# Expert stage of a diffusion block: the order of TensorE's work written by hand, the second product one expert late

## The chip, the cores and the metric

One core of one Trainium2 chip runs the whole kernel as one program. The metric is the device time of one execution in microseconds (us); lower is better. "The time before" is the median of three runs.

## The reference, cut to what matters

One layer: a token mixer for 256 tokens of width 1024 (its code is left out, the change doesn't touch it), then a mixture of 32 experts in which each token goes to 4, and a last norm. All weights are float32; each expert has `w1` (1024 x 2048, 8 MB) and `w2` (1024 x 1024, 4 MB), so that the stage reads 384 MB from HBM.

```python
def moe_ffn(h, w_router, b_router, w1, b1, w2, b2):
    ...
    top_logit, top_e = lax.top_k(logits, TOP_K)
    top_w = jax.nn.softmax(top_logit, axis=-1)
    ...
    def expert_block(args):
        xblk, e = args
        z = xblk @ w1[e] + b1[e]
        gate = jnp.minimum(z[:, :D_EXPERT], SWIGLU_LIMIT)
        lin = jnp.clip(z[:, D_EXPERT:], -SWIGLU_LIMIT, SWIGLU_LIMIT)
        return (gate * jax.nn.sigmoid(SWIGLU_ALPHA * gate) * (lin + 1.0)) @ w2[e] + b2[e]
    ...
    out = jnp.zeros((n_tok + 1, d), hf.dtype).at[slot_tok].add(
        (y * slot_w[:, None]).astype(hf.dtype))[:n_tok]
...
        x = x + g2 * moe_ffn(modulate(x, norm2_g[layer], sh2, sc2), *ffn_w)
    return rms_norm(x, final_g)
```

## The kernel before

The expert stage begins at about 504 us of the profile, after the mixer and the router. The loop of line 879 runs over the 32 experts; each has 64 token slots. For one expert:

- `gather` (lines 762 to 775): a product of the tokens with a 0/1 matrix (`select`) puts the expert's tokens in its slots, transposed, in two halves (`k4`). It is made for two experts at once, so a half is 16 matmul instructions; DVE and ACT move it from PSUM to `xT2` with scale and shift.
- `spread` (lines 777 to 783): one small product and a compare make the matrix `pT` that takes slots back to tokens.
- `expert_in` (lines 785 to 813): the bias of `w1` opens the banks `gate` and `lin` (line 791); eight weight tiles of 1 MB are loaded (line 795) and multiplied (line 798); the clamped SwiGLU runs on DVE and ACT (lines 803 to 807); TensorE turns the result by four transposes (line 810), and ACT copies it to `hT2` (line 812).
- `expert_out` (lines 815 to 843): the bias opens `py` (line 820), four tiles of `w2` are loaded (line 824) and multiplied (line 828), DVE makes `y` (line 831), and for each half `tt` of the tokens a product scatters it (line 840) and DVE adds it to `acc` (line 843). The last expert goes through `expert_out_by_columns` (lines 845 to 866), 256 columns of `w2` at a time (rows of 1 KB), and the final norm follows (lines 958 to 969).

A matmul in float32 is two MATMUL instructions in the profile, and `w1` and `w2` are multiplied in pairs on the two column halves of the array, so one 1 MB tile is 8 instructions for `w1` and 8 for each of the two rows of tiles (`k`) of a `w2` tile.

Order: the kernel is written in Tile, which places all semaphores. Each engine runs its own instructions in order, and that order is made by Tile's planner, from a timeline that it simulates; nothing of it is written by hand in this stage. All weight loads are issued on SP's queue (hardware DMA). Their buffers are a ring of 8 KB a partition (`wtile`, line 45): 3 + 7 + 5 pool buffers and `d0` to `d3` are 19, with `big1` as a twentieth for the first lap alone, as `acc` takes its place; `d0` and `d1` leave the ring at the last two experts (line 881). A load can be issued when TensorE has read the buffer's last content.

PSUM's eight banks: `sc0`, `sc1`, `py` one each, `gate` two, `lin` two, `misc` one (line 750).

Of the kernel before, what the change touches and what calls it, by code (L numbers as in the profile page):

```python
# [8 lines left out]
F32 = mybir.dt.float32  # L9
# [7 lines left out]
P = 128  # L17
# [14 lines left out]
def kernel(  # L32
# [41 lines left out]
    def rstd_of(dst, ss, scale, tmp):  # L74
        """dst = (ss * scale + EPS) ** -0.5: a first guess from the exponent, then Newton steps."""
# [106 lines left out]
    def mod_sums(j, h):  # L182
        """Columns 512 h.. of part j for c, in two steps; still to be summed over partitions."""
# [65 lines left out]
    def modulation(q, w0=None):  # L249
        """md[:, j, a] = columns 256 q.. of part j (shift, scale) for c (a = 0) and c_ctx; a1 = (1 + scale) norm1_g"""  # L250
# [35 lines left out]
    class Granule:  # L286
        """256 columns of a (1024, n) matrix; pieces of k are split into two exact float32r parts."""
# [97 lines left out]
    def pair_dense(j, iv, q, og, sg):  # L385
        """The dense products of two heads, a granule a step."""
# [19 lines left out]
    def decays(hd, k, q):  # L406
        """The decayed queries and keys of a head; in [channel, token]."""
# [41 lines left out]
    def attend(hd, dec, iv, og):  # L449
        """Scores and states, output, and its norm and gate: three steps."""  # L450
# [299 lines left out]
    for tags, bufs in ((("sc0", "sc1", "py"), 1), (("gate",), 2), (("misc",), 1), (("lin",), 2)):  # L750
# [26 lines left out]
    def spread(sel, slot0):  # L777
        """[64 h + s, t] = 1 where token t has slot s + slot0 with the selected expert"""
# [6 lines left out]
    def expert_in(xT, selb, w1e):  # L785
        """swiglu(x w1 + b1) of the 64 tokens of xT; [channel, kt % 4, 64 (kt // 4) + slot]"""
# [20 lines left out]
        ve.scalar_tensor_tensor(l, l, 1.0, g, op0=OP.add, op1=OP.mult)  # L807
        ph = bank2("misc", (P, 4, P))
# [6 lines left out]
    def expert_out(hT2, pT, selb, wcol, w2e, old=None):  # L815
        """acc = old + wcol * pT^T (g2 * (h w2 + b2))"""
# [14 lines left out]
        ve.tensor_mul(y, py, g2h)  # L831
        nonlocal acc
# [4 lines left out]
        for tt in range(2):  # L837
# [7 lines left out]
    def expert_out_by_columns(hT2, pT, selb, wcol, w2e):  # L845
        """The same, 256 columns at a time, with what the final norm needs of them; halves of py hold partial sums."""
        selb = selb.to_broadcast([96, C])
        for j in range(4):
            s = slice(j * 256, (j + 1) * 256)
            w = wtile([P, KT, 256])  # L850
            nc.sync.dma_start(w, w2e[:, s].rearrange("(k p) n -> p k n", p=P))
            py = bank2(("py", "misc")[j % 2], (P, 256))
            te.matmul(py[0:C], selb, b3[:, 2, s], start=True, stop=False, skip_group_check=True)
            for kt in range(KT):
                h = kt % 2
                te.matmul(py[h * C:(h + 1) * C], hT2[:, kt % 4, (kt // 4) * C:(kt // 4) * C + C], w[:, kt],
                          start=kt == 1, stop=kt >= KT - 2, skip_group_check=True)
            y = wk.tile([P, 256], F32, name="y")
            ve.tensor_mul(y, py, g2bc[:, s])
            for tt in range(2):  # L860
# [5 lines left out]
                (gp if j < 3 else ve).tensor_mul(accg[:, tt, s], acc[:, tt, s], fgbc[:, s])  # L866

    xT2 = p2 = None

    def expert_rows(e, n):  # L870
        """Selects and gathers for n experts from e."""
        m = e % 2
        for k in range(n):
            for tt in range(2):
                select(p2[:, tt, m + k], posm[:, tt, e + k:e + k + 1], tt)
# [132 lines left out]
```

## Time and profile before

| | before |
|---|---|
| time, median of three runs (lowest to highest) | 1496.63 us (1494.55 to 1498.79) |
| span of the profiled execution, first to last instruction | 1494.2 us |
| time less span | 2.4 us |
| TensorE (PE) busy | 1371.3 us (92%) |
| VectorE (DVE), ScalarE (ACT), GpSimd (POOL) busy | 640.2, 308.1, 162.2 us |
| moved by DMA | 487.44 MB, mean 326 GB/s |

The profile is of one execution of its own; its span is the sum that the prediction is made against, and what lies around the span (launch and end) is in the time alone. Busy time of an engine is the union of its instructions; "PEld" is the loading of TensorE's stationary operand, which overlaps its matmuls. A trace lacks a few per cent of the matmul records, so counts of matmuls can be some short. "<-" in a wait names what ended it.

### The profile page before, as it was taken

The numbers are of one execution on the slowest core, as the hardware profiler recorded it, in microseconds if no ns is written. First come the engines' busy times: TensorE is split into PE (matmuls) and PEld (weight loads), VectorE is DVE, ScalarE is ACT, GpSimd is POOL, SyncE is SP. The second block draws the span as 40 slices with busy tenths as digits, with TensorE's granted clock in tenths as the row PEclk, the third lists the DMA queues.
The fourth block names the chain that finished last, engine by engine and source line by source line (L and its number), as shares of the span: only waits on it lengthen the run. The fifth ranks groups of instructions, "written<-read, shape, count | busy, mean of one in ns | idle before, by whom it ended". The sixth has DMA issues, their size and how long they took to land. (4 is left out here: it accounts for less than half of the span.)

```text
span 1494.2 us, 19672 instructions
## 1 busy us (share of the span) xinstructions
PE 1371.3 (92%) x8218; PEld 760.8 (51%) x8218; DVE 640.2 (43%) x1108; ACT 308.1 (21%) x497; POOL 162.2 (11%) x109
## 2 busy tenths in 40 slices
PE   6979797979999989999999999998999989998996
PEld 4979797979999633343333233333333333333233
DVE  5598879697787421322323222222222222222124
ACT  3463535373444200000000000000000000001001
POOL 3054414240171000000000000000000000000001
PEclk8999999999999999999999999999999999999998
DMA  9536243435977799999999999999999999999970
GB/s 334 186 101 220 101 158 113 152 131 171 345 249 300 308 377 377 416 414 419 416 416 418 416 416 418 418 416 416 418 418 416 415 417 411 414 410 413 388 276 30
DMA packets 146560, 487.44 MB, mean 326 GB/s; under 512 B 9097, under 2 KB 71682, under 8 KB 113698
## 3 DMA queue, kind: packets, MB, share of 16 engines
q1 hardware_dynamic: 145618, 483.37, 83.1%
q0 software_dynamic: 848, 2.75, 0.6%
q8 instruction: 67, 1.10, 0.3%
q14 instruction: 27, 0.22, 0.0%
HBM read 485.04 MB, written 1.05 MB: 325 GB/s over the span
## 5 line engine op out<-in xcount | busy, mean ns | idle before, releaser
L798 PE MATMUL gate<-w,xT 128*64 128x512 f32 x1024 | 271.0, 598 | 4.0 <-DVE xT L775 4.0
L798 PE MATMUL lin<-w,xT 128*64 128x512 f32 x1024 | 272.1, 592 | 0.0
L828 PE MATMUL py<-w,hT 128*64 128x512 f32 x992 | 243.4, 634 | 16.1 <-ACT hT L812 16.1
L321 PE MATMUL acc<-hh,ghi 128*128 128x256 f32 x576 | 166.9, 290 | 12.1 <-ACT iv L394 12.1
L321 PE MATMUL acc<-hh,glo 128*128 128x256 f32 x576 | 165.5, 288 | 11.3 <-DVE glo L242 11.3
L321 PE MATMUL acc<-hl,ghi 128*128 128x256 f32 x576 | 165.1, 287 | 0.0
L242 DVE TENSOR_TENSOR glo<-w,ghi 128x1024 fp32r<-128x1024 f32 (+1 forms) x99 | 140.0, 1419 | 50.7 <-ACT ghi L241 50.3
L798 PEld LDWEIGHTS lin<-w,xT 128*64 128x64 f32 x1024 | 75.4, 137 | 148.4 <-issue 148.2
L828 PEld LDWEIGHTS py<-w,hT 128*64 128x64 f32 x992 | 71.2, 143 | 143.8 <-issue 115.9
L843 DVE SCALAR_TENSOR_TENSOR acc<-sc,wts,acc 128x512 f32<-128x512 f32 x124 | 89.0, 747 | 123.5 <-PE sc L840 123.4
L798 PEld LDWEIGHTS gate<-w,xT 128*64 128x64 f32 x1024 | 69.4, 136 | 127.1 <-issue 106.6
L241 ACT ACTIVATE ghi<-w 128x1024 fp32r<-128x1024 f32 (+1 forms) x102 | 102.3, 1007 | 144.6 <-PE acc L321 107.7
L321 PEld LDWEIGHTS acc<-hh,ghi 128*128 128x128 f32 x576 | 111.4, 194 | 13.3 <-ACT iv L394 12.5
L321 PEld LDWEIGHTS acc<-hh,glo 128*128 128x128 f32 x576 | 111.3, 193 | 12.9 <-DVE glo L242 12.6
L803 DVE TENSOR_SCALAR g<-gate 128x512 f32<-128x512 f32 x32 | 22.1, 692 | 212.1 <-PE gate L798 202.3
L321 PEld LDWEIGHTS acc<-hl,ghi 128*128 128x128 f32 x576 | 111.4, 193 | 0.7 <-issue 0.7
L804 ACT ACTIVATE s<-g 128x512 f32<-128x512 f32 x32 | 20.2, 630 | 423.6 <-DVE g L803 423.6
L884 POOL DMA_DIRECT2D bc<-in_final_g_dram x1 | 0.6, 557 | 934.7 <-DMA w<-in_w_dram 934.7
L831 DVE TENSOR_TENSOR y<-py,g2h 128x512 f32<-128x512 f32 x31 | 21.4, 692 | 165.0 <-PE py L828 165.0
L840 PE MATMUL sc<-y,pT 64*128 64x512 f32 x248 | 84.7, 641 | 8.0 <-DVE y L831 7.8
L321 PE MATMUL acc<-ghi,hh 128*128 128x256 f32 x256 | 73.3, 288 | 13.8 <-DVE og L383 6.3
L321 PE MATMUL acc<-glo,hh 128*128 128x256 f32 x256 | 73.1, 286 | 1.4 <-DVE glo L242 1.4
(320 smaller groups left out, 1656.1 us busy)
## 6 DMA issues: line engine op xcount, KB each, us to landing
w<-in_w_dram SPq DMA_DIRECT2D x384, 1024.0 KB, 13.7
w<-in_w_in_dram SPq DMA_DIRECT2D x33, 1024.0 KB, 5.7
w<-in_w_mod_dram SPq DMA_DIRECT2D x24, 1024.0 KB, 6.9
w<-in_w_branch_a_dram SPq DMA_DIRECT2D x4, 1024.0 KB, 16.3
w<-in_w_branch_b_dram SPq DMA_DIRECT2D x4, 1024.0 KB, 12.2
w<-in_w_out_dram SPq DMA_DIRECT2D x4, 1024.0 KB
w<-in_w_in_dram SPq DMA_DIRECT2D x12, 256.0 KB, 7.7
bt<-in_b_dram POOLq DMA_DIRECT2D x9, 128.0 KB, 5.0
```

Source lines behind the costliest of these rows:

```text
L241: sc.activation(hi, src, AF.Copy)
L242: eng.tensor_sub(lo, src, hi)
L321: te.matmul(o, l, r, start=opens and kt == 0 and n == 0, stop=kt == KT - 1 and n == 2, skip_group_check=True)
L798: te.matmul(zz[n][h * C:(h + 1) * C], xT[:, kt], w[:, n * D + h * 512:n * D + (h + 1) * 512], start=False, stop=kt == KT - 1, skip_group_c ...
L803: ve.tensor_scalar(g, zz[0], 7.0, None, op0=OP.min)
L804: sc.activation(s, g, AF.Sigmoid, scale=1.702)
L828: te.matmul(py[h * C:(h + 1) * C], hT2[:, kt % 4, (kt // 4) * C:(kt // 4) * C + C], w[:, k, h * 512:(h + 1) * 512], start=False, stop=kt = ...
L831: ve.tensor_mul(y, py, g2h)
L840: te.matmul(pcs[h], pT[h * C:(h + 1) * C, tt * P:(tt + 1) * P], y[h * C:(h + 1) * C], start=True, stop=True)
L843: ve.scalar_tensor_tensor(acc[:, tt, s], pcs[h], wcol[tt], old[:, tt, s], op0=OP.mult, op1=OP.add)
L884: gp.dma_start(fgbc, bcast(final_g, D))
```

## The change

- TensorE's order in the expert stage is the program's own (`manual_schedule` for that engine); the other engines are still planned.
- In the turn of expert e, TensorE does: the opening of `gate` and `lin`; the eight steps of `w1` (0 to 7), with the scatter of expert e-2 after the steps 1 and 2 (one token half each) and, in odd turns, the gather for e+1 and e+2 after the steps 3 and 5 (one half each; in turn 0 the gather for expert 1); then `spread` and the second product of expert e-1; then the transposes of expert e. SwiGLU of e runs on DVE and ACT meanwhile.
- PSUM: `gate` and `lin` have one bank each, `misc` three, and both halves of the gather go to `misc`.
- Last expert: as before in 256 columns, but the scatter of a column follows the product of the next; `d0` and `d1` leave the ring one expert later.
- Loads are issued in the order of the new program: `w1` of e, then `w2` of e-1.

The fallback for an expert with more than 64 tokens (line 921) is rewritten with the same pieces; it doesn't run with these inputs. Comments that the diff removes are left out here.

```diff
-    for tags, bufs in ((("sc0", "sc1", "py"), 1), (("gate",), 2), (("misc",), 1), (("lin",), 2)):
+    for tags, bufs in ((("sc0", "sc1", "py"), 1), (("gate",), 1), (("misc",), 3), (("lin",), 1)):
...
-    def gather(tok, xT, n):
-        for k4 in range(2):
-            pg = bank2(("misc", "sc0")[k4], (P, 4, n))
+    def gather(tok, xT, n, k4s=(0, 1)):
+        for k4 in k4s:
+            pg = bank2("misc", (P, 4, n))
             for k in range(4):
                 kt = 4 * k4 + k
                 for tt in range(2):
...
-    def expert_in(xT, selb, w1e):
+    def w1_open(selb):
         zz = [bank2("gate"), bank2("lin")]
...
-        for kt in range(KT):
-            w = wtile([P, 2 * D])
-            nc.sync.dma_start(w, w1e(kt))
-            for n in range(2):
-                for h in range(2):
-                    te.matmul(zz[n][h * C:(h + 1) * C], xT[:, kt], w[:, n * D + h * 512:n * D + (h + 1) * 512],
-                              start=False, stop=kt == KT - 1, skip_group_check=True)
+        return zz
+    def w1_step(zz, xT, kt, src):
+        w = wtile([P, 2 * D])
+        nc.sync.dma_start(w, src)
+        for n in range(2):
+            for h in range(2):
+                te.matmul(zz[n][h * C:(h + 1) * C], xT[:, kt], w[:, n * D + h * 512:n * D + (h + 1) * 512],
+                          start=False, stop=kt == KT - 1, skip_group_check=True)
+    def swiglu(zz):
...
+        return l
+    def turned(l):
...
-    def expert_out(hT2, pT, selb, wcol, w2e, old=None):
+    def w2_steps(hT2, selb, w2e):
         selb = selb.to_broadcast([96, C])
         py = bank2("py")
...
         y = wk.tile([P, 512], F32, name="y")
         ve.tensor_mul(y, py, g2h)
+        return y
+    def scatter(y, pT, wcol, old=None, tts=(0, 1)):
...
-        for tt in range(2):
+        for tt in tts:
             pcs = [bank2(f"sc{h}") for h in range(2)]
...
-    def expert_out_by_columns(hT2, pT, selb, wcol, w2e):
+    def last_columns(j, hT2, pT, selb, wcol, w2e):
         selb = selb.to_broadcast([96, C])
-        for j in range(4):
-            s = slice(j * 256, (j + 1) * 256)
...
+        s = slice(j * 256, (j + 1) * 256)
+        w = wtile([P, KT, 256])
+        nc.sync.dma_start(w, w2e[:, s].rearrange("(k p) n -> p k n", p=P))
...
+        y = wk.tile([P, 256], F32, name="y")
+        ve.tensor_mul(y, py, g2bc[:, s])
+        def rest():
             for tt in range(2):
                 pc = bank2((("sc0", "sc1"), ("gate", "lin"))[j % 2][tt], (P, 256))
...
+        return rest
-    def expert_rows(e, n):
...
-    for e in range(E):
...
+    tok, xTs = {}, {}
+    def rows_of(e, n):
         if e % 2 == 0:
             p2 = wk.tile([P, 2, 2, C], F32, name="p2")
             xT2 = wk.tile([P, KT, 2 * C], F32, name="xT2")
+            for k in range(2):
+                tok[e + k], xTs[e + k] = p2[:, :, k], xT2[:, :, k * C:(k + 1) * C]
+        else:
+            p2, xT2 = tok[e], xTs[e]
+        for k in range(n):
             for tt in range(2):
+                select(tok[e + k][:, tt], posm[:, tt, e + k:e + k + 1], tt)
+        if n == 2:
+            t, x = p2.rearrange("p t a b -> p t (a b)"), xT2
+        else:
+            t, x = tok[e], xTs[e]
+        return [lambda k4=k4: gather(t, x, n * C, (k4,)) for k4 in range(2)]
+    w1e = lambda e, kt: w1[0, e, kt * P:(kt + 1) * P]
+    w2e = lambda e: lambda k2: w2[0, e, k2 * 256:(k2 + 1) * 256]
+    sel = lambda e: sel96[:, e:e + 1]
+    wcols = lambda e: [wts[:, tt, e:e + 1] for tt in range(2)]
+    out_of = ready = None
+    with tc.manual_schedule(engines={mybir.EngineType.PE}):
+        first_zz = w1_open(sel(0))
+        for f in rows_of(0, 1):
+            f()
+        for e in range(E):
...
+            if e == E - 1:
+                slots[:] = [x for x in slots if x[1] not in ("d0", "d1")]
+                bc = consts.tile([P, 2, D], F32, name="bc", tag="d0")
+                fgbc, g2bc = bc[:, 0], bc[:, 1]
+                gp.dma_start(fgbc, bcast(final_g, D))
+                accg = consts.tile([P, 2, D], F32, name="accg", tag="d1")
+                ss8 = consts.tile([P, 2, 4], F32, name="ss8")
+            zz = w1_open(sel(e)) if e else first_zz
+            for kt in range(KT):
+                w1_step(zz, xTs[e], kt, w1e(e, kt))
+                if kt in (1, 2) and ready:
+                    scatter(*ready[1:], x1 if ready[0] == 0 else None, (kt - 1,))
+                if kt == 3:
+                    steps = rows_of(1, 1) if e == 0 else rows_of(e + 1, 2) if e % 2 and e < E - 1 else []
+                if kt in (3, 5) and steps:
+                    steps[kt // 2 - 1]()
+                if e == E - 1 and kt in (3, 5):
+                    pb = bank2("misc")
+                    h = kt // 2 - 1
+                    te.matmul(pb, ident[:, h * C:h * C + 1].to_broadcast([P, P]), g2h, start=True, stop=True)
+                    sc.activation(g2bc[:, h * 512:(h + 1) * 512], pb, AF.Copy)
+            l = swiglu(zz)
+            if out_of:
+                pe, phT = out_of
+                pT = spread(identb[:, pe:pe + 1], 0)
+                y = w2_steps(phT, sel(pe), w2e(pe))
+                ready = pe, y, pT, wcols(pe)
+            out_of = e, turned(l)
+        e, hT2 = out_of
         pT = spread(identb[:, e:e + 1], 0)
+        rest = last_columns(0, hT2, pT, sel(e), wcols(e), w2[0, e])
+        scatter(*ready[1:])
+        for j in range(1, 4):
+            then = last_columns(j, hT2, pT, sel(e), wcols(e), w2[0, e])
+            rest()
+            rest = then
+        rest()
 
```

## Rows read from the trace of the kernel before

**Rows 1.** The page: the span, and the busy time of the engines.

```profile
span 1494.2 us, 19672 instructions
...
PE 1371.3 (92%) x8218; PEld 760.8 (51%) x8218; DVE 640.2 (43%) x1108; ACT 308.1 (21%) x497; POOL 162.2 (11%) x109
```

**Rows 2.** Stretches of the expert stage: from and to, length, busy time of PE, PEld, DVE, ACT, POOL (with instructions), then TensorE's granted clock, the DMA engines' busy share and GB/s.

```profile
508.80:600.00 91.20, 86.64 (x397) 32.56 (x398) 18.72 (x39) 8.23 (x16) 0.00 (x0) 0.96 0.98 378
600.00:700.00 100.00, 99.17 (x466) 39.30 (x464) 30.98 (x56) 8.57 (x16) 0.00 (x0) 1.00 1.02 417
...
1300.00:1400.00 100.00, 91.73 (x423) 32.31 (x425) 25.98 (x44) 6.43 (x12) 0.56 (x1) 0.98 1.00 403
...
1434.00:1450.00 16.00, 15.09 (x79) 6.06 (x77) 3.98 (x7) 2.14 (x4) 0.00 (x0) 1.00 1.00 335
```

**Rows 3.** The DMA table of the stretch 600 to 1300 us, the queue that carries the weights: packets, MB, share of the 16 engines' time. Under it, what SP's queue waited for (total us, times, longest): first in 508 to 600 us, then in 600 to 900 us.

```profile
q1 hardware_dynamic: 51828, 290.95, 101.5%
...
SPq L795 <- PE lin L798: 28.6, 14, 4.7
...
SPq L795 <- DMA w<-in_w_dram: 60.4, 42, 2.2
```

**Rows 4.** The loads of expert weights on SP's queue issued up to 503 us (count, duration of the issue, first and last start, and the time from issue to landing), and then the last four of the stage, with the landing times of the loads of 1400 to 1450 us.

```profile
L795 SPq DMA_DIRECT2D w<-in_w_dram x16: 327/334/729, 436.2 to 502.5; - x16
L824 SPq DMA_DIRECT2D w<-in_w_dram x4: 378/379/397, 459.0 to 471.2; - x4
DMA to landing us min/median/max: 4.7/5.9/10.4
...
L851 SPq DMA_DIRECT2D w<-in_w_dram x4: 367/368/1582, 1434.7 to 1442.5; - x4
...
DMA to landing us min/median/max: 5.8/6.7/7.2
```

**Rows 5.** The timeline of the end: start, length, engine, line, operation, tiles, shape, count, and in brackets the idle time before and what ended it. Two additions behind a scatter half; the last column group's product; the scatter that follows it.

```profile
1469.67 1.41 DVE L843 SCALAR_TENSOR_TENSOR acc<-sc,wts,acc 128x512 f32<-128x512 f32 x2 [1.22 <-PE sc L840]
...
1479.34 2.01 PE L856 MATMUL misc<-w,hT 128*64 128x256 f32 x16
...
1481.29 1.13 PE L862 MATMUL sc<-y,pT 128*128 128x256 f32 x4
```

**Rows 6.** TensorE's timeline of two experts at 661 to 713 us, from one opening of the banks to the next but one.

```profile
661.10 0.39 PE L791 MATMUL gate<-b,sel 96*64 96x512 bf16 x2
...
661.53 1.03 PE L798 MATMUL gate<-w,xT 128*64 128x512 f32 x4
...
665.06 7.03 PE L828 MATMUL py<-w,hT 128*64 128x512 f32 x31
672.02 0.28 PE L780 MATMUL misc<-posT,identb 32*128 32x256 bf16 x1
...
712.39 0.39 PE L791 MATMUL gate<-b,sel 96*64 96x512 bf16 x2
```

**Rows 7.** The same at 1160 to 1223 us.

```profile
1160.77 0.41 PE L791 MATMUL gate<-b,sel 96*64 96x512 bf16 x2
1161.63 0.41 PE L791 MATMUL lin<-b,sel 96*64 96x512 bf16 x2 [0.45 <-DVE l L805]
1162.96 0.66 PE L810 MATMUL misc<-ident,l 128*128 128x128 f32 x4 [0.92 <-DVE l L807]
1164.30 1.94 PE L828 MATMUL py<-w,hT 128*64 128x512 f32 x8 [0.69 <-ACT hT L812]
...
1207.32 1.03 PE L798 MATMUL gate<-w,xT 128*64 128x512 f32 x4
...
1209.14 1.13 PE L840 MATMUL sc<-y,pT 64*128 64x512 f32 x4
1210.20 1.08 PE L798 MATMUL gate<-w,xT 128*64 128x512 f32 x4
...
1211.96 1.03 PE L798 MATMUL gate<-w,xT 128*64 128x512 f32 x4
...
1213.68 1.03 PE L798 MATMUL gate<-w,xT 128*64 128x512 f32 x4
...
1222.37 0.41 PE L791 MATMUL gate<-b,sel 96*64 96x512 bf16 x2
```

**Rows 8.** The timeline of the beginning: TensorE's first step of `w1`; the issue of the twenty-first load on SP's queue; the first operation of the first SwiGLU; the second product behind it. Last, the stretch 520 to 530 us in the columns of Rows 2.

```profile
508.83 1.08 PE L798 MATMUL gate<-w,xT 128*64 128x512 f32 x4
...
510.81 5.88 SPq L824 DMA_DIRECT2D w<-in_w_dram  x4
...
522.33 0.69 DVE L803 TENSOR_SCALAR g<-gate 128x512 f32<-128x512 f32 x1 [7.40 <-PE gate L798]
...
526.60 8.78 PE L828 MATMUL py<-w,hT 128*64 128x512 f32 x32 [0.69 <-ACT hT L812]
...
520.00:530.00 10.00, 7.94 (x34) 2.73 (x32) 2.67 (x4) 1.23 (x2) 0.00 (x0) 0.85 1.02 421
```

**Rows 9.** TensorE's timeline at 693 to 697 us: a step of `w1` (8 instructions from its start to the next row's), a gather half, and the start of the next step.

```profile
693.04 1.08 PE L798 MATMUL gate<-w,xT 128*64 128x512 f32 x4
...
694.91 2.05 PE L769 MATMUL sc<-p,acc 128*128 128x128 f32 x16
696.89 1.08 PE L798 MATMUL gate<-w,xT 128*64 128x512 f32 x4
```

More of the change, by code (lines that the diff above doesn't have):

```diff
@@ L843, in expert_out @@
                 ve.scalar_tensor_tensor(acc[:, tt, s], pcs[h], wcol[tt], old[:, tt, s], op0=OP.mult, op1=OP.add)
-    def expert_out_by_columns(hT2, pT, selb, wcol, w2e):
+    def last_columns(j, hT2, pT, selb, wcol, w2e):
         selb = selb.to_broadcast([96, C])
-        for j in range(4):
-            s = slice(j * 256, (j + 1) * 256)
[L850 to L859, printed above, removed]
+        s = slice(j * 256, (j + 1) * 256)
+        w = wtile([P, KT, 256])
+        nc.sync.dma_start(w, w2e[:, s].rearrange("(k p) n -> p k n", p=P))
+        py = bank2(("py", "misc")[j % 2], (P, 256))
+        te.matmul(py[0:C], selb, b3[:, 2, s], start=True, stop=False, skip_group_check=True)
+        for kt in range(KT):
+            h = kt % 2
+            te.matmul(py[h * C:(h + 1) * C], hT2[:, kt % 4, (kt // 4) * C:(kt // 4) * C + C], w[:, kt],
+                      start=kt == 1, stop=kt >= KT - 2, skip_group_check=True)
+        y = wk.tile([P, 256], F32, name="y")
+        ve.tensor_mul(y, py, g2bc[:, s])
+        def rest():
             for tt in range(2):
@@ L866, in expert_out_by_columns @@
                 (gp if j < 3 else ve).tensor_mul(accg[:, tt, s], acc[:, tt, s], fgbc[:, s])
-    xT2 = p2 = None
-    def expert_rows(e, n):
[L872 to L875, printed above, removed]
-        gather(p2[:, :, m:m + n].rearrange("p t a b -> p t (a b)"), xT2[:, :, m * C:(m + n) * C], n * C)
-    late = []
-    for e in range(E):
-        if e == E - 2:
-            slots[:] = [x for x in slots if x[1] not in ("d0", "d1")]
-            bc = consts.tile([P, 2, D], F32, name="bc", tag="d0")
-            fgbc, g2bc = bc[:, 0], bc[:, 1]
-            gp.dma_start(fgbc, bcast(final_g, D))
-            for h in range(2):
-                pb = bank2("misc")
-                te.matmul(pb, ident[:, h * C:h * C + 1].to_broadcast([P, P]), g2h, start=True, stop=True)
-                sc.activation(g2bc[:, h * 512:(h + 1) * 512], pb, AF.Copy)
-            accg = consts.tile([P, 2, D], F32, name="accg", tag="d1")
-            ss8 = consts.tile([P, 2, 4], F32, name="ss8")
+        return rest
+    tok, xTs = {}, {}
+    def rows_of(e, n):
         if e % 2 == 0:
@@ L905 @@
-        es = e % 2
-        selb = sel96[:, e:e + 1]
-        pT = spread(identb[:, e:e + 1], 0)
-        hT2 = expert_in(xT2[:, :, es * C:(es + 1) * C], selb, lambda kt: w1[0, e, kt * P:(kt + 1) * P])
-        late.append((hT2, pT, selb, [wts[:, tt, e:e + 1] for tt in range(2)]))
-        if e == E - 2:
-            continue
-        for i, args in enumerate(late):
-            ee = e - len(late) + 1 + i
-            if ee == E - 1:
-                expert_out_by_columns(*args, w2[0, ee])
-            else:
-                expert_out(*args, lambda k2: w2[0, ee, k2 * 256:(k2 + 1) * 256], None if ee else x1)
@@ new lines @@
+    w1e = lambda e, kt: w1[0, e, kt * P:(kt + 1) * P]
[8 more added lines that the diff above has]
+        for e in range(E):
+            if e == 0:
+                ve.tensor_sub(lg, lg, view(top, 0, [[8, 2], [0, E]]))
+                sc.activation(lg, lg, AF.Exp)
+                ve.tensor_mul(wts, lg, mk)
+                ve.reduce_sum(den, wts, axis=mybir.AxisListType.X)
+                ve.reciprocal(den, den)
+                for tt in range(2):
+                    ve.tensor_scalar(wts[:, tt], wts[:, tt], den[:, tt:tt + 1], None, op0=OP.mult)
+            if e == E - 1:
[6 more added lines that the diff above has]
+            zz = w1_open(sel(e)) if e else first_zz
+            for kt in range(KT):
+                w1_step(zz, xTs[e], kt, w1e(e, kt))
[18 more added lines that the diff above has]
+        e, hT2 = out_of
+        pT = spread(identb[:, e:e + 1], 0)
+        rest = last_columns(0, hT2, pT, sel(e), wcols(e), w2[0, e])
[5 more added lines that the diff above has]
+        rest()
@@ L946 @@
                 pT = spread(one[:E], C * blk)
-                hT2 = expert_in(xT, one[:96], lambda kt: w1[0, bass.ds(er, 1), kt * P:(kt + 1) * P]
-                                .rearrange("a p n -> (a p) n"))
-                expert_out(hT2, pT, one[:96], [pw[:, 1, tt:tt + 1] for tt in range(2)],
-                           lambda k2: w2[0, bass.ds(er, 1), k2 * 256:(k2 + 1) * 256].rearrange("a p n -> (a p) n"))
+                zz = w1_open(one[:96])
+                for kt in range(KT):
+                    w1_step(zz, xT, kt, w1[0, bass.ds(er, 1), kt * P:(kt + 1) * P].rearrange("a p n -> (a p) n"))
+                y = w2_steps(turned(swiglu(zz)), one[:96], lambda k2: w2[0, bass.ds(er, 1), k2 * 256:(k2 + 1) * 256]
+                             .rearrange("a p n -> (a p) n"))
+                scatter(y, pT, [pw[:, 1, tt:tt + 1] for tt in range(2)])
         for tt in range(2):
```

11 lines of the change are left out of this document (removed).

## The prediction

> **What bounds the kernel now.** The page comes first: TensorE is busy for 1371.3 of 1494.2 us [rows 1], which looks like an engine at its limit. But that is a mean over two stages, so I went on to the stretches of the expert stage alone [rows 2]: from 600 us on the DMA engines are busy all the time and move 417 GB/s. The DMA table gives the finer figure: 290.95 MB in 700 us are 415.6 GB/s [rows 3], so a tile of 1 MB (1.0486 million bytes) takes 2.523 us, and an expert's twelve tiles 30.3 us. Third view, TensorE's own timeline: two experts take 712.39 - 661.10 = 51.3 us where it never waits [rows 6], but 1222.37 - 1160.77 = 61.6 us later on [rows 7], 30.8 us an expert. So the two limits lie side by side, and the one that decides is a TensorE that needs 26 us an expert, takes 30.8 and so is just slower than the loads. Fourth, the queue of SP: at the beginning it waits for TensorE to give buffers back, and the loads run at 378 GB/s; in 600 to 900 us it waits most for earlier loads [rows 2, 3]; from 1300 us the rate falls to 403 [rows 2]. What that adds up to stands at the end: the last load is issued at 1442.5 us and lands about 5.8 us later, at 1448.3 [rows 4], but TensorE ends the last column product at 1481.3 [rows 5]. It runs 33 us behind data that lie ready. That is what can be won; beyond it the DMA is the floor.
>
> **The change part by part.**
>
> *Second product one expert late.* Removed is the stop at each expert's end: TensorE waits 0.45 us to reopen `lin`, 0.92 us for SwiGLU's result, 0.69 us for its turned copy [rows 7], together 2.06 us. After such a stop the granted clock is also lower: 0.85 over the ten us around the first one, whose second product takes 8.78 us for 32 instructions, where 31 at full clock take 7.03 [rows 8, 6]; some 1.5 us more. In the new order the SwiGLU of e, 2.2 us from the end of `w1` to the transposes (1162.96 - 1160.77) [rows 7], lies under the second product of e-1, which is about 7 us [rows 6], and the copy `hT2` under the next `w1`. Only turn 0 has no such cover: there 2.9 us are waited and a lower clock follows, once.
>
> *What TensorE still does in an expert*, from starts to starts: eight steps of `w1` at 1.72 (1213.68 - 1211.96) [rows 7], 13.8; `w2`, as many instructions, half as many tiles, 6.9; the opening 0.43 (661.53 - 661.10) and `spread` and the bias of `py` 0.4, an estimate by the opening's halves [rows 6]; two scatter halves at 1.06 (1210.20 - 1209.14) [rows 7], 2.1; a gather half at 1.98 (696.89 - 694.91) [rows 9], two for two experts, 2.0; transposes 0.6, by their length [rows 7]. A step before another kind of product takes 1.87 (694.91 - 693.04) [rows 9] instead of 1.72, 0.15 more; five such changes make 0.75. Sum: 27.0 us an expert. The two experts without a wait took 25.6 each [rows 6], so I take 27.0 as the careful one. Either is under the 30.3 us of the loads by 3 us or more.
>
> The changes of kind are where a rule speaks against this order, which cuts `w1` into four or five pieces. The row prices one at 0.15 us. The Trainium skill, TensorEngine Tiling, section Key Properties, says that changing the tiling mode drains the array; if a drain cost a whole matmul's length of 0.6 us, an estimate, five would be 3.0 us and the expert 29.2. That is still under the loads.
>
> *Scatter and gather between the steps.* They are the same instructions as before, moved under nothing. What the trace doesn't show is the wait that they may bring: the second half of a scatter needs `sc0` and `sc1`, whose two additions take 1.41 us on DVE [rows 5]. They are done some 2.6 us after the first half's start (1.06 + 0.1 + 1.41), and the second half's turn comes at 1.06 + 1.87 = 2.9. So 0.3 us cover them; if DVE is late with other work, up to 1.1 us an expert are lost, and behind that wait stand the rest of `w1` and so the return of buffers. A gather waits likewise for `select`. Bounds: 0 and about 2 us an expert for both; I take 0, since DVE is idle over half the time [rows 1] and those two experts at 661 us went through the same kinds of work without a stop.
>
> *Banks.* One `gate` and one `lin` mean that the opening for e+1 waits for DVE's reading of e; that is over some 5 us earlier, behind the second product. Nothing.
>
> *Queues.* SP's loads change only in order (`w1` of e, then `w2` of e-1), which is the order in which TensorE reads, so no load stands before one that is needed sooner. POOL's one load (`final_g`) and the two products for `g2bc` come an expert later; they are needed by the last columns alone. Nothing.
>
> *Last expert in columns.* Before, the scatter already follows the next column's product (1481.29 behind 1479.34) [rows 5]. Nothing, give or take 1 us.
>
> **The sum.** With TensorE at 27 us, the loads decide. Twenty tiles are issued by 502.5 us [rows 4]; the twenty-first can go when the first buffer has been read, at 510.8 [rows 8]. From there 360 tiles at 2.523 us are 908.3 us. The four column loads run at 335 GB/s [rows 2], 3.13 us each, 12.5. From the end of a transfer to its landing: 4.7 (shortest) less 2.5, so 2.2 [rows 4]. In turn 0 the loads run dry: TensorE is done with the first `w1` (with the gather in it) at 508.8 + 13.8 + 4.0 + 0.6 = 527.2, and gives the next buffer back only after the uncovered stop, the transposes, the opening and a slow step, near 534; the eight buffers before that keep the DMA busy for 20.2 us from 510.8, until 531. With what follows I take 5 us lost; bounds 0, and the 8.3 us that the first stretch lost before (378 for 416 in 91 us) [rows 2]. Last landing: 510.8 + 908.3 + 12.5 + 2.2 + 5 = 1438.8.
>
> Then TensorE: the last column's product, 1481.29 - 1479.34 = 1.95 us [rows 5], and a lag of some 1.3 us, since four columns, the scatter of expert 30 with its bank wait and two scatters of columns (some 12.7 us) stand against 9.4 us between the first column's landing and the last's, and 2 us of them are the last product itself. The product ends at 1442.0. From there to the end the kernel before took 1494.2 - 1481.3 = 12.9 us [rows 1, 5], and that part is unchanged: 1454.9. The median lies 2.4 us above the profiled span, so the time is 1457 us. Of the gain of 39, 9.5 come from the earlier last landing (1448.3 to 1438.8) and 30 from a TensorE that is no longer behind.
>
> **Rivals.**
>
> *TensorE is freed only in part.* The bank wait, `select`, or a DVE queue that the planner fills by its own model cost more than I think. At p us an expert the last product ends at 508.8 + 32p + 5.6 (columns in place of a `w2`); this overtakes the loads from p = 29.0. At 29.5 it is 1458.4, the time 1474. For: the cover of 0.3 us is thin. Against: two experts at 25.6 [rows 6]. Chance 0.13, from 1467 to 1490.
>
> *Nothing comes of it* (the order by hand has stops of its own that add up to the old 30.2 us an expert, or isn't the order that runs): 1496. Against it stand the same rows. Chance 0.06.
>
> *The loads are slower than 416 GB/s, and it is slower than before.* In the first stretch the engines are 0.98 busy at 378 GB/s [rows 2]: busy, yet 9% less is moved. If a TensorE that reads each tile as it lands had that effect throughout, a tile would take 2.774 us, 360 of them 90 us more: 1547. It is as slow as before from 2.63 us a tile (398 GB/s). For: nobody waits for data in this trace, so that state isn't in it. Against: in that stretch SP was waiting for buffers [rows 3], which a faster TensorE gives back sooner. Chance 0.06.
>
> *The clock.* TensorE will wait 2.52 - 1.72 = 0.8 us for each tile, and stops have lowered its clock [rows 8]. If the lower level held, 20.7 us of products would double, an expert would take 47.7 us and the kernel some 2050. It can't hold long: at that level a step takes 3.4 us, more than a tile's load, the waiting ends, and with it what lowered the clock. So it costs the tail 2 to 3 us at most, or I misread it: chance 0.03. This is the rule of the Trainium skill, TensorE: Matmul & The Clock Gate, section HAM oscillation: products that wait for DMA at every step start each of them at the lower clock. The trace shows the fall after a stop and the recovery within one product.
>
> **How the numbers follow.** Forecast 1457, chance 0.72, by itself 1447 (no loss in turn 0, no lag, 417 GB/s or a little more) to 1467 (8.3 us lost there, more lag, a slow clock in the tail). The range of 1447 to 1480 adds two thirds of the first rival: 0.80. A measurement of this kernel can tell 0.3%, 4.5 us. Faster by more: 0.72 + 0.13 = 0.85; within: 0.06; slower: 0.06 + 0.03 = 0.09.
>
> **What would show it.** Right: stops between `w1` and `w2` gone; SP's queue waiting for loads, not for TensorE, in most of the stage; TensorE waiting for weights from about 800 us on, some 3 us an expert; the last load issued near 1420 us, and the last column product within 4 us of the last landing. Wrong: SP still waiting for TensorE after 700 us, a stop before the second scatter half or a gather, under 410 GB/s while TensorE waits, or a granted clock under 0.9 over the stage.

## The result, and the profile after

The changed kernel takes 1460.1 us (median of four runs, 1457.56 to 1461.54) against 1497.7 for the kernel before, run on the same chip: a ratio of 0.9762, 95% interval 0.973 to 0.9793. Forecast were 1457 us and a range of 1447 to 1480. The profiled execution has a span of 1455.8 us (its time 1457.56), against 1454.9 in the sum.

The page of the changed kernel: span and busy times.

```profile
span 1455.8 us, 19634 instructions
...
PE 1346.6 (92%) x8218; PEld 739.8 (51%) x8218; DVE 637.2 (44%) x1108; ACT 307.7 (21%) x497; POOL 161.7 (11%) x109
```

TensorE is busy for 92% of the span as before [rows 1]; that number says nothing of what happened. The stretches do (columns of [rows 2]):

```profile
508.80:600.00 91.20, 89.08 (x457) 35.46 (x455) 24.80 (x52) 10.87 (x20) 0.00 (x0) 1.00 0.99 402
...
700.00:800.00 100.00, 100.00 (x486) 35.32 (x484) 28.73 (x52) 7.65 (x14) 0.00 (x0) 1.00 1.02 417
...
1300.00:1400.00 100.00, 90.15 (x415) 28.73 (x411) 22.05 (x35) 6.11 (x11) 0.56 (x1) 1.00 1.02 417
...
1424.00:1440.00 16.00, 14.07 (x83) 7.14 (x80) 5.83 (x11) 1.62 (x5) 1.41 (x2) 1.00 0.72 235
...
530.00:540.00 10.00, 10.00 (x58) 4.81 (x55) 0.82 (x2) 0.91 (x2) 0.00 (x0) 1.00 0.88 322
540.00:550.00 10.00, 10.00 (x54) 3.92 (x54) 4.58 (x11) 1.54 (x3) 0.00 (x0) 1.00 0.97 376
```

In 700 to 800 us TensorE has no pause at all; later it has some, and the loads still move 417 GB/s in 1300 to 1400 us, where the kernel before fell to 403. TensorE's timeline gives the pace by the openings of `gate`: two experts without a wait, the first wait for a tile of weights, and two later experts.

```profile
660.00 0.41 PE L791 MATMUL gate<-b,sel 96*64 96x512 bf16 x2
...
713.69 0.41 PE L791 MATMUL gate<-b,sel 96*64 96x512 bf16 x2
...
833.56 1.08 PE L800 MATMUL gate<-w,xT 128*64 128x512 f32 x4 [0.64 <-DMA w<-in_w_dram]
...
942.01 0.41 PE L791 MATMUL gate<-b,sel 96*64 96x512 bf16 x2
...
1002.42 0.41 PE L791 MATMUL gate<-b,sel 96*64 96x512 bf16 x2
```

(713.69 - 660.00) / 2 = 26.85 us an expert, against the 27.0 of the sum; (1002.42 - 942.01) / 2 = 30.2 later on, which is the loads' pace. What TensorE waited for from 505 to 1443 us, all but 1.0 us (us in total, times, longest):

```profile
PE py L836 <- DMA w<-in_w_dram: 25.8, 44, 1.1
PE gate L800 <- DMA w<-in_w_dram: 21.3, 49, 1.0
PE misc L818 <- DVE l L811: 2.1, 1, 2.1
```

The stops of [rows 7] are gone, but for one in turn 0; what is left are weights. SP's queue from 600 to 1400 us now waits for earlier loads first (451 us over all its lines, 98 before) and for TensorE second (150 us, 557 before). The largest line of each kind:

```profile
SPq L797 <- DMA w<-in_w_dram: 241.0, 149, 2.7
...
SPq L797 <- PE lin L800: 66.5, 40, 3.9
```

The end, in TensorE's timeline: first column product, the second scatter half of expert 30, last column product, its scatter.

```profile
1429.28 1.95 PE L867 MATMUL py<-w,hT 128*64 128x256 f32 x16 [0.21 <-ACT hT L820]
...
1433.12 1.78 PE L852 MATMUL sc<-y,pT 64*128 64x512 f32 x4 [0.84 <-DVE acc L855]
...
1440.87 2.02 PE L867 MATMUL misc<-w,hT 128*64 128x256 f32 x16
1442.82 1.13 PE L875 MATMUL sc<-y,pT 128*128 128x256 f32 x4
```

The last weights move at about 1437 us, and the last column product ends at 1442.8, 5.7 us behind. By the same measure it was 29 us before: the weights' queue still moved a few packets until about 1452 us, and the product ended at 1481.3 [rows 5]. The queue's table of the kernel before, 1451 to 1452 us:

```profile
q1 hardware_dynamic: 22, 0.02, 6.6%
```

### The profile page after: what moved, and what is told of

It reads as the page before. It is cut to its first block, busy times and chain, and to the rows that moved or that the text cites. A ratio compares the mean times of both kernels' runs of the same rounds, so it can differ in the third digit from the quotient of the medians.

```text
span 1455.8 us, 19634 instructions
## 1 busy us (share of the span) xinstructions
PE 1346.6 (92%) x8218; PEld 739.8 (51%) x8218; DVE 637.2 (44%) x1108; ACT 307.7 (21%) x497; POOL 161.7 (11%) x109
## 3 DMA queue, kind: packets, MB, share of 16 engines
HBM read 485.04 MB, written 1.05 MB: 334 GB/s over the span
## 5 line engine op out<-in xcount | busy, mean ns | idle before, releaser
L800 PE MATMUL lin<-w,xT 128*64 128x512 f32 x1024 | 263.5, 592 | 0.0
L836 PE MATMUL py<-w,hT 128*64 128x512 f32 x992 | 228.6, 598 | 26.7 <-DMA w<-in_w_dram 25.8
L836 PEld LDWEIGHTS py<-w,hT 128*64 128x64 f32 x992 | 66.1, 136 | 169.3 <-issue 94.5
L800 PEld LDWEIGHTS gate<-w,xT 128*64 128x64 f32 x1024 | 60.4, 135 | 168.6 <-issue 95.0
L773 ACT ACTIVATE xT<-misc,sh,a 128x128 f32<-128x128 f32 (+1 forms) x68 | 30.7, 451 | 273.4 <-DVE xT L775 273.4
L775 DVE TENSOR_SCALAR xT<-misc,a,sh 128x128 f32<-128x128 f32 (+1 forms) x68 | 27.2, 400 | 130.9 <-PE misc L769 120.4
```

The source lines that it names most:

```text
L773: sc.activation(xT[:, kt], pg[:, k], AF.Identity, bias=sh2[:, kt:kt + 1], scale=a2[:, kt:kt + 1])
L775: ve.tensor_scalar(xT[:, kt], pg[:, k], a2[:, kt:kt + 1], sh2[:, kt:kt + 1], op0=OP.mult, op1=OP.add)
```

## The experiments

The theory: TensorE alone needs 27 us an expert, so that it works off its lag and the loads set the end. The rivals: the order by hand itself brings the gain, or the banks do, or TensorE has a limit of its own near the loads' 30 us. planner_order, same_turn, gather_twice, gather_thrice and w2_kept ran once each; the changed kernel's own runs spread over 4 us.

**planner_order**: the changed program, TensorE's order left to the planner.

```diff
...
-    with tc.manual_schedule(engines={mybir.EngineType.PE}):
+    with nullcontext():
```

> The changed program, but TensorE's order is the planner's again. Theory: the gain came from filling the stops between w1 and w2; the program now offers the second product of the expert before as filling, but the planner decides by its own timeline. If the lateness in the program is enough, the span stays within 6 us of 1456. Rival: the order by hand is what counts, the planner makes stops of about 2 us at the transposes again, and the span is 1480 to 1500.

Measured: 1455.9 us. The order by hand isn't needed: in the program's new order, and with the new banks, the planner finds as good a one.

**same_turn**: the order by hand, but the second product right behind its own SwiGLU.

```diff
-            if out_of:
-                pe, phT = out_of
-                pT = spread(identb[:, pe:pe + 1], 0)
-                y = w2_steps(phT, sel(pe), w2e(pe))
-                ready = pe, y, pT, wcols(pe)
-            out_of = e, turned(l)
+            if e < E - 1:
+                pT = spread(identb[:, e:e + 1], 0)
+                y = w2_steps(turned(l), sel(e), w2e(e))
+                ready = e, y, pT, wcols(e)
+            else:
+                out_of = e, turned(l)
...
-        scatter(*ready[1:])
```

> The order by hand stays, but the second product is no longer one expert late: transposes and w2 of e follow the SwiGLU of e at once. Theory (the stops held the kernel back): each expert waits about 2.2 us for SwiGLU and 0.7 us for the turned copy and loses up to 1.5 us to a lower clock after it, so TensorE's own 26.85 us an expert become 30 to 31.3, near or above the loads' 30.3: span 1470 to 1525, and SP's queue waits for TensorE again. Rival (what held it back was the planner's loads and scatters, not the stops): span within 6 us of 1456.

Measured: 1511.0 us, above the 1492.8 of the kernel before beside it. A wait of TensorE (505 to 1440 us), one of SP (600 to 1400 us), and a stretch:

```profile
PE misc L818 <- DVE l L811: 70.4, 30, 2.4
...
SPq L797 <- PE py L836: 270.2, 105, 7.6
...
1000.00:1100.00 100.00, 92.19 (x421) 31.61 (x417) 24.10 (x41) 5.51 (x10) 0.00 (x0) 0.95 1.01 413
```

With the stop in each turn TensorE decides again, and its granted clock falls to 0.95. In this order nothing stands between SwiGLU and what needs it, and without the lateness the order by hand loses, in spite of the new banks.

**gather_twice, gather_thrice**: each gather product made two or three times over, so that TensorE gets some 2 or 4 us an expert more to do.

```diff
-                for tt in range(2):
+                for tt in (0, 1) * 2:
```

> Each gather product is made twice (the second overwrites the first with the same values), 4.0 us more of TensorE in two experts, 2.0 in one: 28.85 us an expert instead of 26.85. Theory (the loads are the bound, TensorE has 3.4 us an expert to spare): span within 3 us of 1456, TensorE's waits for weights fall by about 60 us in total at most. Rival (TensorE's pace still decides): 62 us more, span about 1518.

> Each gather product is made three times, 4.0 us more of TensorE an expert: 30.85 us, just over the loads' 30.3. Theory (the loads are the bound up to 30.3 us an expert): TensorE becomes the bound, its last product ends at 505 + 32 x 30.85 + 5.6 = 1498, span about 1511, waits for weights near zero. Rival (TensorE's pace decides all along): 124 us more than 1456, about 1580.

Measured: 1468.7 and 1519.5 us. The first lies some 9 us above the changed kernel instead of at it. Its stretches:

```profile
508.80:600.00 91.20, 89.08 (x482) 39.41 (x482) 20.92 (x42) 9.22 (x17) 0.00 (x0) 1.00 0.92 356
600.00:700.00 100.00, 100.00 (x517) 40.19 (x517) 27.46 (x51) 7.97 (x15) 0.00 (x0) 1.00 1.02 416
```

From 600 us on the loads keep 416 GB/s, so the 2 us are hidden there. But in the first 91 us they run at 356 instead of 402: 91.2 x 46 / 416 = 10 us. There the ring is full and a load goes when TensorE gives a buffer back, and three gathers (for expert 0 ahead of the first step, for expert 1, for 2 and 3) are made twice in it or just ahead of it. My forecast counted TensorE's spare time as one sum over the stage, and it isn't: at the beginning there is none. The pace of the two kernels' TensorE where it doesn't wait, by the openings of `gate`, first of gather_twice, then of gather_thrice; behind them the first gather of gather_thrice and a stretch in it:

```profile
735.21 0.41 PE L791 MATMUL gate<-b,sel 96*64 96x512 bf16 x2
...
792.47 0.41 PE L791 MATMUL gate<-b,sel 96*64 96x512 bf16 x2
```

```profile
708.68 0.41 PE L791 MATMUL gate<-b,sel 96*64 96x512 bf16 x2
...
769.51 0.41 PE L791 MATMUL gate<-b,sel 96*64 96x512 bf16 x2
...
503.03 19.45 PE L769 MATMUL misc<-p,acc 128*128 128x64 f32 x96 [0.20 <-DVE p L760]
...
510.00:520.00 10.00, 10.00 (x49) 10.00 (x48) 0.69 (x2) 0.81 (x2) 0.00 (x0) 0.50 0.17 67
```

That is 28.6 and 30.4 us an expert. In gather_thrice TensorE never waits for a weight, so it is the bound throughout. That its span, 1517.7 us, lies within 7 us of the forecast is partly luck: the pace is 0.45 us an expert lower than was taken, 14 us over the stage, and the beginning costs more than was taken, in part because that first gather runs at the lower clock, 0.50.

**w2_kept**: `w2` of the experts 0 to 30 isn't loaded; two tiles that are kept, in buffers taken from the ring, are multiplied in its place.

```diff
-            w = wtile([P, 2, D])
-            nc.sync.dma_start(w, w2e(k2).rearrange("(k p) n -> p k n", p=P))
+            if len(kept) < 2:
+                w = consts.tile([P, 2, D], F32, name="w", tag=f"d{2 + k2}")
+                nc.sync.dma_start(w, w2e(k2).rearrange("(k p) n -> p k n", p=P))
+                kept.append(w)
+            w = kept[k2 % 2]
```

> The changed kernel, in which the `w2` of the experts 0 to 30 isn't loaded: two tiles that are loaded once are multiplied in its place (the output isn't the reference's), so that a turn loads 8 MB instead of 12 and does all of TensorE's work. Theory (TensorE needs 27 us an expert and the loads decide): now TensorE decides; 26.85 us by its pace before 800 us, 32 of them and 5.6 us of the columns from a first step near 507: last column product near 1371, span near 1385, time 1380 to 1395, granted clock 1.00 over the stage. Rival (TensorE has a limit of its own near the 30.2 us that it shows after 800 us): 1470 to 1485.

Measured: 1385.6 us, span 1383.8. A stretch of the middle:

```profile
1100.00:1200.00 100.00, 100.00 (x496) 36.72 (x494) 28.16 (x52) 8.56 (x16) 0.00 (x0) 1.00 0.81 311
```

In this stretch TensorE is never idle and the DMA engines are, at 0.81, and its pace is 26.8 us an expert to the end (`gate` opens at 552.61 us for expert 2 and at 1304.15 for expert 30). So TensorE has no limit near 30 us; in the changed kernel the loads hold the end up by some 72 us.

**late_old_banks** and **banks_only**: the two parts by themselves. The first is the changed kernel with the old banks and the gather in `misc` and `sc0`, the second the kernel before with this edit:

```diff
-    for tags, bufs in ((("sc0", "sc1", "py"), 1), (("gate",), 2), (("misc",), 1), (("lin",), 2)):
+    for tags, bufs in ((("sc0", "sc1", "py"), 1), (("gate",), 1), (("misc",), 3), (("lin",), 1)):
...
-            pg = bank2(("misc", "sc0")[k4], (P, 4, n))
+            pg = bank2("misc", (P, 4, n))
```

> The changed kernel with the banks of before: two for `gate`, two for `lin`, one for `misc`, and the gather's second half in `sc0`. Theory (the lateness of the second product brings the gain, and the banks were taken at nothing): the single `misc` serves a gather half, `spread` and the transposes one after the other, but with some 7 us of other products between any two; TensorE has 3 us an expert to spare against the loads from 600 us on, so the time is within 4 us of the changed kernel's 1459. Rival (the three `misc` banks and the free `sc0` carry part of the gain): TensorE waits for a bank in each turn by 1 us or more, its pace before 800 us is 28 us or more an expert instead of 26.85, the first 90 us of the stage lose further, and the time is 1465 to 1475.

> The kernel before with the banks of the change alone (`gate` and `lin` one each, `misc` three, the gather in `misc`); its order stays the planner's and the second product follows its own SwiGLU. Theory (the stop at an expert's end is what costs): the stop stays, since the transposes still wait for SwiGLU; with one `gate` and one `lin` the opening of the next expert waits in the same stop or goes behind it; 1485 to 1505, within 10 us of the kernel before. Rival (banks held TensorE up): 1455 to 1475.

Measured: 1460.5 us (0.9775, 0.9728 to 0.9821) and 1458.0 us (0.9764, 0.9716 to 0.9813). The first is as the theory has it: its `gate` opens at 663.76 and 717.44 us, 26.8 us an expert with the old banks too. The second is a plain miss: the new banks (three for `misc`, one for `gate` and `lin` each, the gather out of `sc0`; which of these it is wasn't separated), with nothing late and nothing by hand, bring all of the gain. Its timeline over two experts, without waits for weights (an opening, the stop behind it, gather and second product, a scatter half and the step behind it, and the next opening but one):

```profile
834.06 0.41 PE L791 MATMUL gate<-b,sel 96*64 96x512 bf16 x2
834.91 0.41 PE L791 MATMUL lin<-b,sel 96*64 96x512 bf16 x2 [0.45 <-DVE l L805]
836.24 0.65 PE L810 MATMUL misc<-ident,l 128*128 128x128 f32 x4 [0.92 <-DVE l L807]
836.73 3.07 PE L769 MATMUL misc<-p,acc 128*128 128x128 f32 x26
839.73 3.65 PE L828 MATMUL py<-w,hT 128*64 128x512 f32 x16
...
852.80 1.13 PE L840 MATMUL sc<-y,pT 64*128 64x512 f32 x4
853.86 1.08 PE L798 MATMUL gate<-w,xT 128*64 128x512 f32 x4
...
891.21 0.41 PE L791 MATMUL gate<-b,sel 96*64 96x512 bf16 x2
```

And more of the timeline of [rows 7], the kernel before with one `misc`: the first piece of a scatter half cut in two, and two waits.

```profile
1178.84 1.12 PE L840 MATMUL sc<-y,pT 64*128 64x512 f32 x2
1179.89 1.08 PE L798 MATMUL gate<-w,xT 128*64 128x512 f32 x4
...
1187.23 1.08 PE L798 MATMUL gate<-w,xT 128*64 128x512 f32 x4 [0.51 <-DVE xT L775]
...
1206.02 1.13 PE L840 MATMUL sc<-y,pT 64*128 64x512 f32 x4 [0.80 <-DVE y L831]
```

The stop for SwiGLU (0.45 and 0.92) is still there in each turn. What changed is the order that the planner makes: with a bank free, a gather goes into the wait for the turned copy, and the waits for `xT` and `y` are gone from this stretch. Over the whole stage (505 us to the end of the products) the waits for the turned copy fall from 16.1 to 4.8 us, those for `xT` from 4.0 to 0 and those for `y` only from 7.8 to 6.3; those for SwiGLU's result stay, 22.2 and 22.8. Two experts take 891.21 - 834.06 = 57.2 us instead of 61.6 [rows 7]. Of these 4.45 us, 2.2 are waits, and 1.05 the scatter half, which before is cut in two pieces that take as long each (1179.89 - 1178.84) as a whole one (853.86 - 852.80); the remaining 1.2 I haven't traced, the cuts in `w1` and `w2` being the likely place. So it is 28.6 us an expert here, and 29.3 over the next eight, which don't wait for weights either (`gate` opens at 891.21 and 1125.47 us); the sum's own break-even was 29.0. The banks alone bring TensorE just to that point: it waits for weights only 11 times in the stage, 5.6 us, where the changed kernel does 93 times.

**before_long_rows**: the kernel before with the load of the next experiment.

> The kernel before with `w2` of the experts 0 to 30 loaded in runs of 8 KB, by which the loads of the changed kernel got 8.3 us faster. Theory (the first claim of the prediction: before, TensorE decides with 30.8 us an expert, and the data lie ready 33 us ahead of it at the end): faster loads bring nothing, the time is within 4 us of the kernel before, and the last landing moves earlier by up to 8 us. Rival (before, too, the loads' 30.3 us an expert set the pace, and the 33 us are a lag from the beginning alone): 6 to 9 us faster, as in the changed kernel.

Measured: 1497.1 us, 1.0019 (0.9995 to 1.0043). Its stretches, and what SP waited for from 1100 to 1400 us:

```profile
900.00:1100.00 200.00, 182.98 (x842) 65.29 (x840) 51.17 (x90) 14.09 (x26) 0.00 (x0) 0.98 1.01 419
1100.00:1200.00 100.00, 92.52 (x419) 33.97 (x417) 24.66 (x46) 7.34 (x14) 0.00 (x0) 0.95 0.99 402
...
SPq L795 <- PE py L829: 85.5, 31, 6.7
```

The loads get faster, fill the ring by 1100 us and then wait for TensorE. So TensorE decided before, as the prediction's first part has it. (The last landing does not come earlier, against the expectation's last clause: the last loads, too, wait for TensorE.)

**w2_long_rows, both_ends, long_rows_ends**: what can be won from loads that decide, beside five more rounds of the changed kernel (**after_again**). In the first, each partition reads two neighbouring rows of `w2` (runs of 8 KB in place of two of 4 KB), and the transposes pick the channels to match. In the second, gather steps for expert 1 cover the stop of turn 0, and the two scatter halves of expert 30 lie around the first column product. The third has both.

```diff
...
-            te.transpose(ph[:, k], l[:, k * P:(k + 1) * P], ident)
+            part = l.rearrange("a (m p k) -> a m k p", m=2, k=2)[:, k // 2, k % 2] if pairs else l[:, k * P:(k + 1) * P]
+            te.transpose(ph[:, k], part, ident)
...
-            nc.sync.dma_start(w, w2e(k2).rearrange("(k p) n -> p k n", p=P))
+            nc.sync.dma_start(w, w2e(k2).rearrange("(p k) n -> p k n", p=P))
...
```

```diff
-                if kt in (3, 5) and steps:
+                if e and kt in (3, 5) and steps:
...
             l = swiglu(zz)
+            if e == 0:
+                for f in steps:
+                    f()
...
+        scatter(*ready[1:], None, (0,))
         rest = last_columns(0, hT2, pT, sel(e), wcols(e), w2[0, e])
-        scatter(*ready[1:])
+        scatter(*ready[1:], None, (1,))
```

> The changed kernel once more, as the yardstick for the three that run beside it: about 37 us faster than before (ratio 0.975).

> The w2 tiles of experts 0 to 30 are read in runs of 8 KB (two neighbouring rows of w2 to a partition) instead of 4 KB; the transposes take every second column to match. In the changed kernel a 1 MB tile takes 2.525 us in the mean; w2 tiles should come down to what w1 tiles take. Theory (the loads are the bound): if runs of 8 KB are 4% faster than two of 4 KB, as the packets of these two sizes are in the trace (314 against 2 x 163 ns), 124 tiles save 0.1 us each, 12 us, ratio to before 0.967. Rival (TensorE is the bound): no change, 0.975.

> Two moves in TensorE's order. Turn 0: the gather for expert 1 goes behind the last step of w1, where it covers the SwiGLU that nothing covers. End: the two scatter halves of expert 30 go ahead of the first column product and behind it, instead of both behind it. Theory: the loads run dry once, in 530 to 550 us, for 3.3 us, since buffers come back late in turn 0, and TensorE reaches the last column 3.5 us after it landed; the moves give 3 and 1.9 us, 5 in all, ratio 0.972. Rival (neither end is on the path): no change.

> Both of the two before together. Theory: the gains add, 12 + 5 = 17 us on the changed kernel, ratio to before 0.964; TensorE's 26.85 us an expert stay under the loads' 29.9. Rival: the tail or TensorE takes a part of it back, under 12 us.

| | us, median of 6 | ratio to before, 95% |
|---|---|---|
| after_again | 1459.1 | 0.9759 (0.972 to 0.9797) |
| w2_long_rows | 1450.8 | 0.9707 (0.9666 to 0.9747) |
| both_ends | 1454.4 | 0.9737 (0.9698 to 0.9777) |
| long_rows_ends | 1445.5 | 0.9676 (0.9633 to 0.9718) |

The weights' queue in 600 to 1300 us, with 4 KB runs (after_again) and with 8 KB runs, and 530 to 550 us of after_again and of both_ends:

```profile
q1 hardware_dynamic: 51962, 291.21, 101.5%
```

```profile
q1 hardware_dynamic: 40364, 293.96, 101.0%
```

```profile
530.00:550.00 20.00, 20.00 (x109) 8.72 (x107) 5.40 (x13) 2.46 (x5) 0.00 (x0) 1.00 0.86 314
```

```profile
530.00:550.00 20.00, 20.00 (x107) 8.57 (x104) 5.52 (x14) 2.46 (x5) 0.00 (x0) 1.00 1.02 415
```

A tile takes 2.497 us instead of 2.520, times 360 is 8.3 us: the whole of what was measured. The 12 us expected came from packet times, which overlap. Turn 0 gives 20 x (415 - 314) / 416 = 4.9 us by these rows. The move at the end is worth 2.0 us by the timelines: from the last transposes to the end of the last column product it is 12.9 us (1425.51 to 1438.43) instead of 14.9 (1429.19 to 1444.08 in after_again). Together that is more than the 4.7 us between the medians and the 5.6 between the two profiles; from the first step of `w1` to the last transposes both_ends is only 4.0 us shorter. So both ends give something, and the split is known to about 1 us. The two experiments add up to 13.0 of the 13.6 of long_rows_ends, the fastest version.

## Why the prediction was right, point by point

*What bounds.* Right, shown from both sides: faster loads alone bring nothing to the kernel before (before_long_rows), and with fewer loads TensorE keeps its own pace to the end (w2_kept). The 33 us behind data that lie ready were some 29: the prediction took the shortest landing time for the last load, and packets of the weights moved until about 1452 us.

*TensorE's 27.0 us.* Measured 26.85 in the changed kernel and over the whole stage of w2_kept. With that pace against 30.2, TensorE gains 3.4 us an expert on the loads; it first waits for a tile at 833 us, in the turn of expert 12, where the prediction had about 800.

The 25.6 us of [rows 6] that stood beside the 27.0 were misread. The planner had put an opening well ahead of its products, so that between the two marks lie only 13 steps of `w1` instead of 16, with a wait of 0.24 us. The products into `gate` between the openings, four to a step, in the kernel before (661.10 to 712.39 us) and in the changed one (660.00 to 713.69):

```profile
L798 PE MATMUL gate<-w,xT 128*64 128x512 f32 x52 | 13.5, 596 | 0.0
```

```profile
L800 PE MATMUL gate<-w,xT 128*64 128x512 f32 x64 | 16.7, 602 | 0.0
```

With three more steps of 1.72 us it would be 56.5 us, some 28 an expert, an estimate from these rows. The sum didn't use the 25.6, but the prediction held them against its first rival.

The rule of the Trainium skill, TensorEngine Tiling (Array Packing), section Key Properties, priced in the prediction at 29.2 us an expert by an estimate of the drain, isn't borne out at that size.

*Second product one expert late.* Right in what it does, but not the only way, and this is what the prediction didn't see: it took the banks as a side condition ("Nothing"), and the banks alone suffice, as lateness alone does. The banks alone bring TensorE to the break-even of 29.0 us (28.6 to 29.3), the lateness alone well under it (26.8); what lies below is hidden behind the loads, so the gains don't add. The number would have come out with either cause, and says nothing about which. gather_twice (28.6) and gather_thrice (30.4) lie on the two sides of that same point.

*Turn 0.* The one stop that was left open is there, 2.1 us where 2.9 were taken. The lower clock behind it came in after_again and not in the profile above. The stretch 520 to 530 us of both, the changed kernel's first profile first:

```profile
520.00:530.00 10.00, 7.88 (x42) 2.70 (x40) 3.89 (x10) 3.32 (x5) 0.00 (x0) 1.00 1.00 415
```

```profile
520.00:530.00 10.00, 7.88 (x32) 2.65 (x32) 4.01 (x10) 3.32 (x5) 0.00 (x0) 0.83 1.01 420
```

*Scatter and gather.* Taken at 0 within 0 to 2 us an expert; measured 0 until the end. The bank wait of 0.84 us comes once, at 1433 us, where the second half has no step of `w1` ahead of it.

*The sum.* The stage began 3.6 us earlier in this profile (505.3 for 508.8). Up to there the kernels differ only in the banks and the order of the first openings and gather, and the kernel before with longer rows began at 507.5, so part of it is scatter; how much the change did isn't traced. From that start, the product of the last column was to end after 933.2 us and did so after 937.6. Of the 4.4 us missed, 0.4 are lag and 4.0 the loads, whose last packets move 931.8 us after the start instead of 927.8. The queue's table from 505.27 to 1440 us has 383.65 MB, 365.9 tiles:

```profile
q1 hardware_dynamic: 71867, 383.65, 100.5%
```

The sum had 364.8: a load that is issued has not yet moved, 2.8 us. The column loads ran at some 285 GB/s (1422 to 1437 us; the 235 over 1424 to 1440 holds 3 us in which next to nothing moves), some 2 us more than at 335. Against that, turn 0 lost 10 x (1 - 322/416) + 10 x (1 - 376/416) = 3.2 us (in after_again 4.9) where 5 were taken, and the tile took 2.520 instead of 2.523, 1.1 less. About 2 us stay untraced. The tail from there was 13.0 us for 12.9. So the agreement of the span, 1455.8 for 1454.9, is partly luck: the earlier start hides a miss of 4 us. And the last load went out at 1426.2 us, not near 1420.

*The rivals.* Freed only in part: no, though it was closer than it looked, as gather_twice shows. Nothing comes of it: no, 1460.1. Slower loads: no, 417 GB/s while TensorE waits. The clock: no. TensorE waits up to 1.1 us for a tile, 93 times, at a granted clock of 1.00 in every stretch from 800 to 1440 us; the fall that the prediction read from the Trainium skill, TensorE: Matmul & The Clock Gate, section HAM oscillation, is not in this trace. same_turn, whose stops last up to 2.4 us, has 0.95 in the stretch shown.

## What to carry to other kernels

Where two limits lie within a few per cent, work out the pace that the slower one must reach to catch up by the end (here 29.0 us an expert), and look for the smallest edit that gets there: two lines on the banks did, just, what a new pipeline did. Beyond that point only the other limit pays, here longer runs and the gaps at both ends of the stage. A ring of buffers hides an engine's extra work only while the ring isn't full: at the start of a stage it costs nearly in full (here 10 us of loads). And where a planner moves instructions, count the work between two marks before taking their distance for a pace.

## What the runs showed of the hardware

- A 1 MB tile takes 2.497 us on average with `w2` in runs of 8 KB, 2.520 with runs of 4 KB (293.96 and 291.21 MB in 700 us), with the DMA engines busy all the time in both.
- A scatter half of four instructions takes 1.06 us in one piece; two of them by themselves take 1.05 as well. So here the two halves of the array worked side by side only where their instructions followed one another.
- Issuing a column load (runs of 1 KB) kept SP's queue for 2.7 to 10.4 us each, where a load landed some 20 us after its issue at the median; in the kernel before it took 0.37 us at the median, with 6.7 us to the landing [rows 4]. Why the issue took so long stays open: no run here varies it by itself.
- In gather_thrice the granted clock fell to 0.50, the lower of its two levels (1.2 GHz), inside a gather in which TensorE was never idle: 96 instructions of 128x64 took 19.45 us, 0.20 each. In turn 0 of the same run 48 of them took 5.57 us, 0.12 each, at 1.00. This was seen in one run; the gathers of the other runs at this place kept 1.00.

The issues of the column loads in the changed kernel (count, shortest, median and longest issue in ns, first and last start):

```profile
L862 SPq DMA_DIRECT2D w<-in_w_dram x4: 2721/3668/10441, 1408.2 to 1426.2; - x4
```
